# A two-layer token mixer with routed experts on one core: the router's ranks and gates for all tiles in one step, and the second layer's first modulation vectors computed behind the first layer's output projection

## The chip, the cores and the metric

One NeuronCore of a Trainium2 chip runs the whole program in one launch. The metric is the time of one execution on the device in microseconds (us), as the median of 3 runs. Engines are named as the profile names them: PE is the matrix engine (PEld its weight load), DVE, ACT and POOL are the vector, scalar and general engines, and SP is the engine whose queue issues every transfer from the chip's memory (HBM) into the on-chip memory (SBUF). Matrix results land in PSUM banks.

## The reference, cut to what matters

There are 256 context tokens and 256 latent tokens of width 1024, in four tiles of 128 tokens, and two layers. A layer first makes six modulation vectors per condition from `silu(c) @ w_mod + b_mod` (a matrix of 1024 x 6144, 24 MB, in chunks of 2048 columns: chunk 0 is shift and scale ahead of the mixer), then mixes tokens (layer 0: mLSTM and retention heads; layer 1: differential attention), projects out, and runs a mixture of experts. The router picks one of 4 groups and two of its 8 experts:

```python
u_lat = adaln(h_lat, norm1_g[l], m_lat[:, 0], m_lat[:, 1])     # chunk 0 of the layer's modulation
h_lat = h_lat + m_lat[:, 2] * y_lat                            # y_lat: the mixer's output projection
pg_top, grp = lax.top_k(softmax(x @ wg + bg), 1)               # one group of 4
pe_top, e_in = lax.top_k(softmax(le[grp]), TOP_K)              # two of its 8 experts
gate = pg_top * pe_top / sum(pe_top)
out[tok] += gate * ((silu(x @ w1[e]) * (x @ w3[e])) @ w2[e])   # 32 experts, 6 MB of weights each
```

All arithmetic is in float32. Each layer reads 192 MB of expert weights.

## The kernel before, in words

The program is written with four engine streams. A scheduler orders the instructions of the mixer stages; in `weave` (L183) a main task and side tasks are interleaved by estimated PE time, which sets the program order that the scheduler starts from. In the expert stages the PE order is the written one (`manual_schedule`). Each engine executes its own stream strictly in order, and so does SP's queue: a transfer that waits holds up all transfers behind it.

**Transfers.** `wslot` (L98) puts every 1 MB weight slice into a buffer of a ring. Ring a has three such buffers, and further rings (b, c, e) open when stages end. The list `slots` names the ring of the next slice. During the whole of layer 0 it is `[0, 0, 0]`, ring a. In the last part of layer 0, one of ring a's three buffers holds `vw`, the float32 router input of the last two tiles, so two are left.

**Modulation.** `mod_gen` (L219) takes eight slices of `w_mod` in turn; each needs four matmuls of 32 rows (`modps`, L226, 8 records in the trace), then one DVE addition of the bias (L230). `mod_cols` (L284) transposes the result (`modtp`) and copies shift and scale into `sh1` and `a11`. In layer 0 the generator `mods0` (L1316) makes chunks 1 and 2 and then chunk 0 of layer 1, one slice after every second step of the dense projections.

**Layer 0's end.** The output projection is done for the second half of the columns with one tile at a time (L1447; `oacc`, L954 to L956), while two tasks `Router.part` (tiles 0 and 1, then 2 and 3) add the result to the stream `h`, transpose it (`hpt`), compute the logits (`lgp`, L523), and pick groups and experts in some 25 short DVE operations (`first_max`) that end in the two-hot matrix `selb` (`go`, L561). `finish` (L580) turns it into ranks: 128x32 matmuls (`rank`) count earlier tokens of the same expert, DVE makes `pos`, and `gates` makes the gates. Tiles 0 and 1 are finished on their own, before tiles 2 and 3 have their logits.

**Experts.** `moe` (L629) prefetches 12 slices, then `prep` (L658) builds the 0/1 matrix `Pm` from `pos`, and `gather` (L670) multiplies it with the tokens to collect each expert's up to 64 tokens (`ga`; tiles 0 and 1 as a high and a low part, L683 and L684; tiles 2 and 3 of the first group of four experts in float32 from `vw`, L680). Before the change, `Pm` and the gather of tiles 0 and 1 for all four banks come first, and tiles 2 and 3 are added when their ranks are there. `up` (L828) multiplies with w1 and w3 (`f`, L844 and L846), with the gathers of banks 2 and 3 between the first expert's halves; `down` multiplies with w2 (`y`, L868), and the result is spread back (`sc`, L714 and L715). Two experts form a pair; 16 pairs make a layer.

Of the kernel before, what the change touches and what calls it, by code (L numbers as in the profile page):

```python
# [11 lines left out]
F32 = mybir.dt.float32  # L12
# [11 lines left out]
CAP = 64  # L24
# [50 lines left out]
def tile_backbone(ctx, tc, x, c, ctx_in, c_ctx, w_mod, b_mod, norm1_g, norm2_g, w_in_even, ml_gate_b,  # L75
# [361 lines left out]
    class Router:  # L437
# [37 lines left out]
        def part(self, i0, tiles, banks, m2, rows, pool, pp, lgp, vh, vl):  # L475
# [2 lines left out]
            m, q = len(tiles), 1 if tiles[0] < 2 else 0  # L478
            last = i0 + m == self.nt
            if i0 == 0:  # L480
                self.selb = go[:, 2:4, :].rearrange("p a b -> p (a b)").bitcast(BF16).rearrange("p (a b) -> p a b", b=32)
# [9 lines left out]
            def st(name, *shape, pool=pool):  # L491
                return pool.tile([128, m] + list(shape), F32, tag=f"r_{name}", name=name)
# [45 lines left out]
            def first_max(src, w, costs, oh, mx, which=ALU.is_equal):  # L538
# [3 lines left out]
                for i in range(m):  # L542
# [7 lines left out]
            eg = st("eg", 4, pool=keep)  # L550
# [8 lines left out]
            sel = gs[:, i0:i0 + m, :]  # L559
            selb = self.selb  # L560
            V.tensor_tensor(selb[:, i0:i0 + m, :], oh1, oh2, op=ALU.add)  # L561
# [3 lines left out]
            e = st("e", pool=keep)  # L565
            V.tensor_tensor(e, m2, m1, op=ALU.subtract)
            S.activation(e, e, AF.Exp)
            self.state = i0, m, sel, eg, e, oh1, oh2
# [10 lines left out]

        def finish(self, rk):  # L580

            i0, m, sel, eg, e, oh1, oh2 = self.state
            selb = self.selb
            last = i0 + m == self.nt
            for i in range(m):
                for q in range(i0 + i):
                    mm(rk[:, i, :], lhsT=ones_b.to_broadcast([128, 128]), rhs=selb[:, q, :], start=(q == 0), stop=False)
                mm(rk[:, i, :], lhsT=stri_b, rhs=selb[:, i0 + i, :], start=(i0 + i == 0), stop=True)
            if last:
                for i in range(self.nt):  # L590
                    mm(rk[:, m, :], lhsT=ones_b.to_broadcast([128, 128]), rhs=selb[:, i, :], start=(i == 0), stop=(i == self.nt - 1))
            gst, post, got = gs[:, i0:i0 + m, :], pos[:, i0:i0 + m, :], go[:, i0:i0 + m, :]
            V.scalar_tensor_tensor(post, rk[:, 0:m, :], 1.0, sel, op0=ALU.add, op1=ALU.mult)
            if last:
                V.tensor_scalar(ovf, rk[:, m, :], CAP + 0.5, None, op0=ALU.is_ge)

            def st(name):
                return keep.tile([128, m], F32, tag=f"r_{name}", name=name)

            def bc(ap):  # L600
                return ap.unsqueeze(2).to_broadcast([128, m, 32])

            def gates():
                zg = st("zg")
                V.tensor_reduce(zg, eg, axis=AX.X, op=ALU.add)
                g1 = st("g1")
                V.scalar_tensor_tensor(g1, e, 1.0, zg, op0=ALU.add, op1=ALU.mult)
                V.reciprocal(g1, g1)
                g2 = st("g2")
                V.tensor_tensor(g2, e, g1, op=ALU.mult)  # L610
                V.tensor_tensor(oh1, oh1, bc(g1), op=ALU.mult)
                V.tensor_tensor(oh2, oh2, bc(g2), op=ALU.mult)
                V.tensor_tensor(gst, oh1, oh2, op=ALU.add)
                V.scalar_tensor_tensor(got, post, CAP + 0.5, gst, op0=ALU.is_ge, op1=ALU.mult)

            if last:
                self.gates = gates
            else:
                gates()

    def row(vec, q, hl, pool, pp, name):

# [6 lines left out]
    def moe(l, tiles, rt, ahead):  # L629
# [25 lines left out]
        once.insert(9, extra.pop(l))  # L655
        once.insert(11, extra.pop())

        def prep(eg, part=slice(0, nt)):  # L658
            es = slice(4 * eg, 4 * eg + 4)
            if part.start == 0:  # L660
                sel[eg] = pool.tile([128, nt, 4, CAP], F32R, tag="Pm", bufs=1, name="Pm")
                xgs[eg] = pool.tile([128, 8, 4 * CAP], F32, tag=f"xg{eg % 2}", bufs=1, name="xg")
            n = part.stop - part.start
            return V.tensor_tensor(sel[eg][:, part], iota.unsqueeze(1).unsqueeze(1).to_broadcast([128, n, 4, CAP]),  # L664
                            pos[:, part, es].unsqueeze(3).to_broadcast([128, n, 4, CAP]), op=ALU.is_equal)

        def bank(shape, name):
            return pp.tile(shape, F32, tag="x", bufs=4, name=name)

        def gather(eg, kk, part=range(nt), pg=None):  # L670

            Pm, xg = sel[eg], xgs[eg]
            if pg is None:
                pg = bank([128, 2, 4 * CAP], "ga")
            for r in range(2):
                k = 2 * kk + r
                for i in part:
                    rhs = Pm[:, i].rearrange("p e s -> p (e s)")
                    if eg == 0 and i >= nt - 2:
                        mm(pg[:, r, :], lhsT=rt.v[:, i - nt + 2, k, :], rhs=rhs.bitcast(F32), start=(i == 0 and r == 0),  # L680
                           stop=(i == nt - 1 and r == 1))
                        continue
                    mm(pg[:, r, :], lhsT=vh[i][:, k, :], rhs=rhs, start=(i == 0 and r == 0), stop=False)  # L683
                    mm(pg[:, r, :], lhsT=vl[i][:, k, :], rhs=rhs, start=False, stop=(i == nt - 1 and r == 1))  # L684
            if nt - 1 in part:
                S.activation(xg[:, 2 * kk:2 * kk + 2, :], pg, AF.Copy)
            return pg

        def gated(p):

# [190 lines left out]

        order = pe_order()
        fetch(12)
        begun = [None] * 4
        if nt == 4:
            prep(0, slice(0, 2))
        rt.finish(pp.tile([128, 3, 32], F32, tag="f1", bufs=2, name="rank"))
        chosen = prep(0, slice(nt - 2, nt))
        if nt == 4:
            begun = [gather(0, kk, range(2)) for kk in range(4)]  # L890
        rt.gates()
        for kk in range(2):
            gather(0, kk, range(nt - 2, nt), begun[kk])
        pend = iter(())
        npair = NEXP // 2
        ng = npair // 2
# [414 lines left out]
    def z0(b):  # L1311
        return [(t0, zh[b], zl[b]) for t0 in (0, 128)]

    msb10 = modp.tile([128, 512], F32, tag="msb", name="msb10")

    def mods0():  # L1316
        yield from mod_gen(0, 1, modp, mpp, "mp", msb1)
        hl = split_rows(wsp, msb1, ("whi", "wlo"), 3)
# [119 lines left out]
    def late_rows():  # L1438
        for q in (1, 0):
# [4 lines left out]
            rows[q] = s2, row(4, q, hl, late, pp, f"a2{q}")  # L1444
            yield 0.5, 0.0, None

    weave(itertools.chain(*(out_proj(W, [(z0(0) + z0(1))[j]], accp, "acc", [banks[j]], kept=kept if j else None,  # L1447
                                     keeps=None if j else kept) for j in range(4))),
          ([late_rows()], 1),
          ([rt.part(0, (0, 1), banks, m2[0], lambda: rows.get(1), late, pp, lgp[:, 0:2], x8(0, 2), x8(2, 2)),  # L1450
            rt.part(2, (2, 3), banks, m2[1], lambda: rows.get(0), late, pp, lgp[:, 2:4], x8(1, 2), x8(3, 2))], 2))
# [264 lines left out]
```

## Time and profile before

| what | us |
|---|---|
| median of 3 runs (1610.06 to 1611.92) | 1611.63 |
| profiled execution, its own time | 1612.89 |
| its span, first to last instruction | 1611.0 |
| PE busy | 1511.6 (94%) |
| DVE busy | 710.4 (44%) |
| ACT busy | 490.3 (30%) |
| the transfers of the issuing queue, as a share of 16 DMA engines' span | 78.0% |

The mean granted PE clock is 0.981 of full speed. In the trace's timeline the layer 0 mixer ends at 383.4 us with the last `oacc` matmul; the first expert stage runs from there to 888, the second layer's mixer to 1120, and the second expert stage to the end. A PE that is shown busy need not be at its peak, since ends of matmuls are modelled: the distance between starts is the better measure. An engine's idle time is shown with what ended it ("<-"). Waits on SP's queue are waits before a transfer was issued; when it lands is read from the stretches in which bytes flow.

### The profile page before, as it was taken

To read this page: it belongs to the slowest core of one execution; us is meant where nothing else is said; L and a number is where in the kernel's file an instruction comes from. 1 tells how busy PE (TensorE), PEld (TensorE's weight loads), DVE (VectorE), ACT (ScalarE), POOL (GpSimd) and SP (SyncE) were. 2 spreads that over 40 slices of the span, in tenths; PEclk is the share of its full clock that TensorE was granted. 3 is DMA by queue.
4 is the path that set the end of the run, shared out by engine and by line. 5 is a ranking of instruction groups with operands and counts; after the bars stand their busy time and mean duration, and the time that the engine had idled before them with its cause. 6 is when DMAs were issued, how large, how long until landed. Compare 5 with 4: busy or idle time off the path is not lost. (4 is left out here: it accounts for less than half of the span.)

```text
span 1611.0 us, 19387 instructions
## 1 busy us (share of the span) xinstructions
PE 1511.6 (94%) x7354; PEld 833.7 (52%) x7354; DVE 710.4 (44%) x1496; ACT 490.3 (30%) x913; POOL 318.8 (20%) x287
## 2 busy tenths in 40 slices
PE   6999999997999999999998899999899999999985
PEld 4676666676545445454443556767434443433432
DVE  2345685577234445344343566565323232322323
ACT  3326563372211111111111567665212111111111
POOL 1100021000024334234243311001012121211212
PEclk9999999998999999999999999999899999999998
DMA  9554435324999999999997765227899999999994
GB/s 321 198 204 163 157 106 183 105 105 181 380 379 420 420 420 419 420 419 420 420 420 296 265 254 170 104 79 288 312 398 420 421 419 420 420 420 421 419 421 166
DMA packets 96682, 498.35 MB, mean 309 GB/s; under 512 B 14132, under 2 KB 22628, under 8 KB 42180
## 3 DMA queue, kind: packets, MB, share of 16 engines
q1 hardware_dynamic: 96580, 497.02, 78.0%
q8 instruction: 61, 1.00, 0.3%
q14 instruction: 41, 0.34, 0.1%
HBM read 495.94 MB, written 1.05 MB: 308 GB/s over the span
## 5 line engine op out<-in xcount | busy, mean ns | idle before, releaser
L846 PE MATMUL f<-w,xg 128*64 128x512 f32 x1024 | 450.8, 594 | 16.5 <-DMA w<-in_w_dram 16.5
L844 PE MATMUL f<-w,xg 128*64 128x512 f32 x1024 | 450.8, 593 | 0.0
L846 PEld LDWEIGHTS f<-w,xg 128*64 128x64 f32 x1024 | 137.6, 137 | 200.8 <-issue 161.0
L717 DVE TENSOR_TENSOR tmp<-sc,m 128x512 f32<-128x512 f32 x192 | 128.2, 688 | 253.8 <-PE sc L715 241.5
L718 POOL TENSOR_TENSOR h_lat<-h_lat,tmp 128x512 f32<-128x512 f32 x124 | 157.5, 1283 | 395.1 <-DVE tmp L717 391.5
L868 PE MATMUL y<-w,gT 128*64 128x512 f32 x1024 | 226.8, 595 | 0.0
L844 PEld LDWEIGHTS f<-w,xg 128*64 128x64 f32 x1024 | 137.8, 137 | 120.8 <-issue 117.7
L848 ACT ACTIVATE g<-f 64x512 f32<-64x512 f32 x64 | 37.9, 592 | 411.4 <-PE f L846 277.2
L395 DVE TENSOR_TENSOR wlo<-w,whi 128x512 fp32r<-128x512 f32 x136 | 98.9, 733 | 124.8 <-ACT whi L394 117.6
L718 POOL TENSOR_TENSOR h_ctx<-h_ctx,tmp 128x512 f32<-128x512 f32 x62 | 85.2, 1386 | 339.1 <-DVE tmp L717 338.0
L868 PEld LDWEIGHTS y<-w,gT 128*64 128x64 f32 x1024 | 70.6, 137 | 133.4 <-issue 131.3
L394 ACT ACTIVATE whi<-w 128x512 fp32r<-128x512 f32 x136 | 88.6, 658 | 144.3 <-PE dacc L426 88.3
L425 PE MATMUL dacc<-x,whi 128*128 128x512 f32 (+1 forms) x320 | 128.0, 403 | 3.9 <-DVE rq L1380 2.5
L849 DVE TENSOR_TENSOR g<-g,f 64x512 f32<-64x512 f32 x64 | 43.8, 685 | 194.5 <-ACT g L848 193.6
L427 PE MATMUL dacc<-x,wlo 128*128 128x512 f32 (+1 forms) x320 | 120.3, 378 | 2.0 <-DVE wlo L395 1.8
L426 PE MATMUL dacc<-x,whi 128*128 128x512 f32 (+1 forms) x320 | 120.0, 375 | 0.0
L878 DVE SCALAR_TENSOR_TENSOR yhl<-y,gsl,yhl 128x1024 fp32r<-128x1024 f32 (+1 forms) x34 | 41.5, 1221 | 138.4 <-ACT yhl L877 136.9
L877 ACT ACTIVATE yhl<-y,gsl 128x1024 fp32r<-128x1024 f32 (+1 forms) x34 | 36.2, 1064 | 205.9 <-PE y L868 204.2
L714 PE MATMUL sc<-yhl,Gm 128*128 128x512 f32 x192 | 83.7, 436 | 12.8 <-issue 12.4
L683 PE MATMUL ga<-Pm,x 128*128 128x256 f32 x352 | 88.7, 287 | 0.3 <-DVE Pm L664 0.3
L684 PE MATMUL ga<-Pm,x 128*128 128x256 f32 x352 | 88.0, 285 | 0.0
L695 DVE TENSOR_SCALAR Pg<-ca,pos,gs 128x64 f32<-128x64 f32 x192 | 79.7, 477 | 5.6 <-PE gg L702 5.6
(355 smaller groups left out, 2148.5 us busy)
## 6 DMA issues: line engine op xcount, KB each, us to landing
w<-in_w_dram SPq DMA_DIRECT2D x384, 1024.0 KB
w<-in_w_mod_dram SPq DMA_DIRECT2D x40, 1024.0 KB
w<-in_w_in_even_dram SPq DMA_DIRECT2D x16, 1024.0 KB
w<-in_w_in_odd_dram SPq DMA_DIRECT2D x12, 1024.0 KB
wm<-in_w_mod_dram SPq DMA_DIRECT2D x16, 512.0 KB
w<-in_w_out_even_dram SPq DMA_DIRECT2D x4, 1024.0 KB
w<-in_w_out_odd_dram SPq DMA_DIRECT2D x4, 1024.0 KB
cb<-in_consts_dram SPq DMA_DIRECT2D x1, 1344.0 KB
```

The lines of the kernel that those rows point to most:

```text
L394: S.activation(hi, w, AF.Copy)
L395: V.tensor_tensor(lo, w, hi.bitcast(F32), op=ALU.subtract)
L425: mm(d, lhsT=hi[:, sl], rhs=ah(k, ts), start=(k == 0), stop=False)
L426: mm(d, lhsT=hi[:, sl], rhs=al(k, ts), start=False, stop=False)
L427: mm(d, lhsT=lo[:, sl], rhs=ah(k, ts), start=False, stop=(k == 7))
L683: mm(pg[:, r, :], lhsT=vh[i][:, k, :], rhs=rhs, start=(i == 0 and r == 0), stop=False)
L684: mm(pg[:, r, :], lhsT=vl[i][:, k, :], rhs=rhs, start=False, stop=(i == nt - 1 and r == 1))
L717: V.tensor_tensor(tmp, sc, m5s[0][:, 1 if j < 2 else 0, hs], op=ALU.mult)
L718: (V if final and half else G).tensor_tensor(h[j][:, hs], h[j][:, hs], tmp, op=ALU.add)
L844: mm(f1[o1:o1 + 64, :], lhsT=xg[:, k, xsl], rhs=wa[:, kk, :], start=(k == 0), stop=(k == 7), tile_position=(0, o1))
L846: mm(f1[o3:o3 + 64, :], lhsT=xg[:, k, xsl], rhs=wb[:, kk, :], start=(k == 0), stop=(k == 7), tile_position=(0, o3))
L868: mm(y[64 * q:64 * q + 64, half, :], lhsT=gT[:, k, 64 * q:64 * q + 64], rhs=ws[q][:, r, 512 * half:512 * half + 512], start=(k == 0), stop ...
```

## The change

Two edits are made. First, the router: `part` no longer calls `finish`, and one `finish` after both parts makes ranks for all four tiles in one PSUM tile, one `pos`, one `Pm` for all tiles, and then the gates of all tiles, which are held behind `Pm` (`issue_after`). The one-hot matrices are written straight into `gs` and into a part of `go`, so that the second sum and some small operations go (12 DVE instructions fewer over both layers). The gather is no longer split into tiles 0 and 1 and tiles 2 and 3. Second, chunk 0 of layer 1's modulation leaves `mods0` and becomes `next_mods`, appended to the main task of the last weave, behind the four output projections.

```diff
         def part(self, i0, tiles, banks, m2, rows, pool, pp, lgp, vh, vl):
-            oh1, oh2 = st("oh1", 32, pool=keep), st("oh2", 32, pool=keep)
+            oh1, oh2 = gs[:, its], self.sec[:, its]
...
-            V.tensor_tensor(sel, oh1, oh2, op=ALU.add)
...
-            if not last:
-                self.finish(pp.tile([128, m + 1, 32], F32, tag="ps", name="rank"))
-                yield 0.4, 0.0, None
...
         def finish(self, rk):
+            nt, selb, eg, e = self.nt, self.selb, self.eg, self.e
+            for i in range(nt):
+                for q in range(i):
                     mm(rk[:, i, :], lhsT=ones_b.to_broadcast([128, 128]), rhs=selb[:, q, :], start=(q == 0), stop=False)
...
+            V.scalar_tensor_tensor(post, rk[:, 0:nt, :], 1.0, selb[:, 0:nt], op0=ALU.add, op1=ALU.mult)
...
         (moe)
-        begun = [None] * 4
-        if nt == 4:
-            prep(0, slice(0, 2))
-        rt.finish(pp.tile([128, 3, 32], F32, tag="f1", bufs=2, name="rank"))
-        chosen = prep(0, slice(nt - 2, nt))
-        if nt == 4:
-            begun = [gather(0, kk, range(2)) for kk in range(4)]
-        rt.gates()
+        rt.finish(pp.tile([128, nt + 1, 32], F32, tag="f1", bufs=2, name="rank"))
+        chosen = prep(0)
+        with tc.issue_after(chosen.ins):
+            rt.gates()
         for kk in range(2):
-            gather(0, kk, range(nt - 2, nt), begun[kk])
+            gather(0, kk)
...
         (mods0)
-        yield from mod_gen(1, 0, modp, mpp, "mp", msb10)
-        mod_cols(1, msb10, pp, "ps", sh1, a11)
-        yield 0.9
...
+    def next_mods():
+        msb = late.tile([128, 512], F32, name="msb10")
+        yield from mod_gen(1, 0, late, accp, "acc", msb)
+        mod_cols(1, msb, pp, "ps", sh1, a11)
+        yield 0.9
+
     weave(itertools.chain(*(out_proj(...) for j in range(4)), next_mods()),
```

On PE, at the end of layer 0's output projection, the rows before were these (`hpt` and `lgp` are the transposes and logits of the last two tiles, `rank` the rank matmuls):

```order
L956 MATMUL oacc<-wk,x_2731 128x512
L588 LDWEIGHTS stri_b
L588 MATMUL rank<-go,stri_b 128x32
L587 LDWEIGHTS ones_b
L587 MATMUL rank<-go,ones_b 128x32
L588 LDWEIGHTS stri_b
L588 MATMUL rank<-go,stri_b 128x32
L511 MATMUL hpt<-ca,h_lat 128x128 x8
L523 MATMUL lgp<-wr,hT 128x36 x8
L587 LDWEIGHTS ones_b
L587 MATMUL rank<-go,ones_b 128x32
```

At the same place on PE the changed kernel has:

```order
L930 MATMUL oacc<-wk,x_2665 128x512
L514 MATMUL hpt<-ca,h_lat 128x128 x4
L526 MATMUL lgp<-wr,hT 128x36 x4
L226 MATMUL modps<-w,cond 32x512 x32
L287 MATMUL modtp<-ca,msb_3228 128x128 x4
L582 LDWEIGHTS stri_b
L582 MATMUL rank<-go,stri_b 128x32
L581 LDWEIGHTS ones_b
L581 MATMUL rank<-go,ones_b 128x32
```

The rank matmuls of tiles 0 and 1 no longer stand ahead of the last tile's `hpt`; all 32 matmuls of the eight modulation slices and their transposes stand between the last logits and the first rank.

On SP's queue, before, the transfers around the end of layer 0 (`w_out_even` is the output projection, `w` from `w_dram` are expert slices; the brackets name the engines whose progress a transfer waits for) were these:

```order
L114 DMA w<-in_w_out_even_dram 128x4x512 [waits DVE_49]
L114 DMA w<-in_w_dram 128x2048 [waits DVE_49,PE_49,Pool_49]
L114 DMA w<-in_w_dram 128x2048 x2
L114 DMA w<-in_w_dram 128x2048 [waits DVE_49,PE_49]
L114 DMA w<-in_w_dram 128x2048 [waits DMAHW5_49,DVE_49]
L114 DMA w<-in_w_dram 128x2048 [waits DMAHW7_49,DVE_49]
L114 DMA w<-in_w_dram 128x2048 [waits DMAHW6_49,PE_49]
L114 DMA w<-in_w_dram 128x2048 [waits PE_49]
```

In the changed kernel SP's queue reads, from the last of the first four expert slices on:

```order
L114 DMA w<-in_w_dram 128x2048 [waits DMAHW3_49,DVE_49,PE_49]
L111 DMA w<-in_w_mod_dram 128x2048 [waits DMAHW4_49,DVE_49]
L111 DMA w<-in_w_mod_dram 128x2048 [waits DMAHW5_49,DVE_49]
L111 DMA w<-in_w_mod_dram 128x2048 [waits DMAHW6_49,DMAHW4_49,PE_49]
L111 DMA w<-in_w_mod_dram 128x2048 [waits DMAHW7_49,DMAHW5_49,PE_49]
L111 DMA w<-in_w_mod_dram 128x2048 [waits DMAHW6_49,DMAHW0_49,PE_49]
L111 DMA w<-in_w_mod_dram 128x2048 [waits DMAHW7_49,DMAHW1_49,PE_49]
L111 DMA w<-in_w_mod_dram 128x2048 [waits DMAHW2_49,DMAHW0_49,PE_49]
L111 DMA w<-in_w_mod_dram 128x2048 [waits DMAHW3_49,DMAHW1_49,PE_49]
L114 DMA w<-in_w_dram 128x2048 [waits DMAHW2_49,PE_49]
L114 DMA w<-in_w_dram 128x2048 [waits DMAHW3_49,PE_49]
L114 DMA w<-in_w_dram 128x2048 [waits DVE_49,Activation_49]
```

The eight modulation slices now stand behind the first four expert slices and ahead of all others. The first two go into the two free buffers of ring a; from the third on, each waits for PE to have multiplied the slice two places before it, and so do the two expert slices that follow.

## Rows read from the trace of the kernel before

**Rows 1.** Stages: busy time by engine (instructions), granted clock, DMA share, rate.
```profile
core 0: us, PE busy (x) PEld busy (x) DVE busy (x) ACT busy (x) POOL busy (x), PEclk, DMA share, GB/s
0.00:383.00 383.00, 364.42 (x1736) 251.18 (x1737) 214.70 (x582) 175.00 (x354) 40.47 (x68) 0.99 0.48 165
400.00:470.00 70.00, 69.78 (x356) 38.47 (x358) 25.04 (x55) 14.43 (x23) 11.00 (x8) 0.96 0.94 372
470.00:850.00 380.00, 379.45 (x1952) 184.58 (x1950) 162.72 (x265) 60.54 (x90) 135.74 (x104) 1.00 1.01 420
1135.00:1611.00 476.00, 437.38 (x2018) 183.57 (x2018) 136.41 (x215) 78.76 (x126) 83.15 (x65) 0.98 0.95 390
```

**Rows 2.** PE's waits, 470 to 850: us in total, times, longest.
```profile
PE gt L855 <- DVE tmp L717: 0.4, 1, 0.4
```

**Rows 3.** PE in time: a modulation slice and the transposes; then their count.
```profile
259.84 1.06 PE L226 MATMUL modps<-w,cond 128*32 128x512 f32 x8
260.83 0.50 PE L430 MATMUL dacc<-whi,x 128*128 128x512 f32 x1
303.51 0.60 PE L287 MATMUL modtp<-ca,msb 128*128 128x128 f32 x4
...
230.00:306.00 76.00, 10.60 (x64) 1.52 (x64) 1.00 0.50 166
```

**Rows 4.** PE in time, from the last output projection to the first expert.
```profile
383.00 0.40 PE L956 MATMUL oacc<-wk,x 128*128 128x512 f32 x1
387.99 1.79 PE L511 MATMUL hpt<-ca,h_lat 128*128 128x128 f32 x8
389.67 1.92 PE L523 MATMUL lgp<-wr,hT 128*128 128x36 f32 x8
399.06 0.18 PE L588 MATMUL rank<-go,stri_b 128*128 128x32 bf16 x1 [4.78 <-DVE go L561]
399.80 0.58 PE L683 MATMUL ga<-Pm,x 128*128 128x256 f32 x1 [0.34 <-DVE Pm L664]
406.12 3.61 PE L680 MATMUL ga<-Pm,vw 128*128 128x256 f32 x16
409.66 0.64 PE L844 MATMUL f<-w,xg 128*64 128x512 f32 x1
416.90 0.64 PE L844 MATMUL f<-w,xg 128*64 128x512 f32 x1
```

**Rows 5.** DVE in time: the last tile's stream, and a `Pm` of all tiles.
```profile
385.95 0.69 DVE L504 TENSOR_TENSOR h_lat<-v,h_lat 128x512 f32<-128x512 f32 x1
417.00 1.23 DVE L664 TENSOR_TENSOR Pm<-ca,pos 128x1024 fp32r<-128x1024 f32 x1 [11.24 <-PE ga L680]
```

**Rows 6.** SP's queue, 330 to 400: an issue, and its waits.
```profile
379.23 4.36 SPq L114 DMA_DIRECT2D w<-in_w_dram  x5
SPq L114 <- PE oacc L956: 39.6, 2, 39.1
```

**Rows 7.** One slice alone: its issue, and the stretch in which it ends.
```profile
304.87 0.37 SPq L114 DMA_DIRECT2D w<-in_w_out_even_dram  x1
309.00:310.00 1.00, 1.00 (x5) 0.75 (x4) 0.25 (x1) 0.69 (x2) 0.00 (x0) 1.00 0.29 109
```

**Rows 8.** Layer 1: three modulation slices after a pause, and SP's wait there.
```profile
892.75 4.48 PE L226 MATMUL modps<-w,cond 128*32 128x512 f32 x24 [4.01 <-DVE tmp L717]
SPq L111 <- PE modps L226: 5.1, 1, 5.1
```

**Rows 9.** Stretches: the clock around the router, and the first expert stage's end.
```profile
390.00:395.00 5.00, 3.54 (x18) 3.34 (x18) 2.09 (x11) 1.51 (x2) 0.00 (x0) 0.50 0.86 362
400.00:405.00 5.00, 5.00 (x24) 5.00 (x25) 5.00 (x19) 0.00 (x0) 0.00 (x0) 0.50 1.01 411
865.00:870.00 5.00, 4.45 (x23) 2.58 (x23) 3.67 (x7) 1.20 (x2) 4.85 (x5) 1.00 0.74 306
```

**Rows 10.** PE in time: the last slices of the first expert stage in use.
```profile
859.39 0.59 PE L846 MATMUL f<-w,xg 128*64 128x512 f32 x1
```

More of the change, by code (lines that the diff above doesn't have):

```diff
@@ L480, in part @@
             if i0 == 0:
-                self.selb = go[:, 2:4, :].rearrange("p a b -> p (a b)").bitcast(BF16).rearrange("p (a b) -> p a b", b=32)
+                self.sec, self.selb = (go[:, n:n + 2, :].rearrange("p a b -> p (a b)").bitcast(BF16)
+                                       .rearrange("p (a b) -> p a b", b=32) for n in (0, 2))
+                self.eg = keep.tile([128, self.nt, 4], F32, tag="r_eg", name="eg")
+                self.e = keep.tile([128, self.nt], F32, tag="r_e", name="e")
             vh, vl = (t.rearrange("p t (k q) -> p t k q", k=8) for t in (vh, vl))
@@ L549, in part @@
             first_max(lg[:, :, 0:4], 4, cost[:, 0:4], ohg, mg, ALU.is_lt)
-            eg = st("eg", 4, pool=keep)
+            its = slice(i0, i0 + m)
+            eg, e = self.eg[:, its], self.e[:, its]
             le = st("le", 32)
@@ L580, in finish @@
         def finish(self, rk):
[L582 to L586, printed above, removed]
-                    mm(rk[:, i, :], lhsT=ones_b.to_broadcast([128, 128]), rhs=selb[:, q, :], start=(q == 0), stop=False)
[L588 to L595, printed above, removed]
+            nt, selb, eg, e = self.nt, self.selb, self.eg, self.e
+            for i in range(nt):
+                for q in range(i):
+                    mm(rk[:, i, :], lhsT=ones_b.to_broadcast([128, 128]), rhs=selb[:, q, :], start=(q == 0), stop=False)
+                mm(rk[:, i, :], lhsT=stri_b, rhs=selb[:, i, :], start=(i == 0), stop=True)
@@ L597, in st @@
+            for i in range(nt):
+                mm(rk[:, nt, :], lhsT=ones_b.to_broadcast([128, 128]), rhs=selb[:, i, :], start=(i == 0), stop=(i == nt - 1))
+            gst, post, got = gs[:, 0:nt], pos[:, 0:nt], go[:, 0:nt]
+            V.scalar_tensor_tensor(post, rk[:, 0:nt, :], 1.0, selb[:, 0:nt], op0=ALU.add, op1=ALU.mult)
             def st(name):
-                return keep.tile([128, m], F32, tag=f"r_{name}", name=name)
-            def bc(ap):
-                return ap.unsqueeze(2).to_broadcast([128, m, 32])
+                return keep.tile([128, nt], F32, tag=f"r_{name}", name=name)
@@ L608, in gates @@
                 V.reciprocal(g1, g1)
[L609 removed]
                 V.tensor_tensor(g2, e, g1, op=ALU.mult)
[L611 to L613 removed]
+                V.tensor_tensor(gst, gst, g1.unsqueeze(2).to_broadcast([128, nt, 32]), op=ALU.mult)
+                for i in range(nt):
+                    V.scalar_tensor_tensor(gst[:, i], self.sec[:, i], g2[:, i:i + 1], gst[:, i], op0=ALU.mult, op1=ALU.add)
@@ L614, in gates @@
                 V.scalar_tensor_tensor(got, post, CAP + 0.5, gst, op0=ALU.is_ge, op1=ALU.mult)
[L616 to L619, printed above, removed]
+            self.gates = gates
     def row(vec, q, hl, pool, pp, name):
@@ L656, in moe, with prep @@
         once.insert(11, extra.pop())
-        def prep(eg, part=slice(0, nt)):
+        def prep(eg):
             es = slice(4 * eg, 4 * eg + 4)
[L660 to L665, printed above, removed]
+            sel[eg] = pool.tile([128, nt, 4, CAP], F32R, tag="Pm", bufs=1, name="Pm")
+            xgs[eg] = pool.tile([128, 8, 4 * CAP], F32, tag=f"xg{eg % 2}", bufs=1, name="xg")
+            return V.tensor_tensor(sel[eg], iota.unsqueeze(1).unsqueeze(1).to_broadcast([128, nt, 4, CAP]),
+                                   pos[:, 0:nt, es].unsqueeze(3).to_broadcast([128, nt, 4, CAP]), op=ALU.is_equal)
@@ L667, in bank, with gather @@
         def bank(shape, name):
             return pp.tile(shape, F32, tag="x", bufs=4, name=name)
-        def gather(eg, kk, part=range(nt), pg=None):
+        def gather(eg, kk):
             Pm, xg = sel[eg], xgs[eg]
-            if pg is None:
-                pg = bank([128, 2, 4 * CAP], "ga")
+            pg = bank([128, 2, 4 * CAP], "ga")
             for r in range(2):
                 k = 2 * kk + r
-                for i in part:
+                for i in range(nt):
                     rhs = Pm[:, i].rearrange("p e s -> p (e s)")
@@ L684, in gather @@
[L684 to L687, printed above, removed]
+                    mm(pg[:, r, :], lhsT=vh[i][:, k, :], rhs=rhs, start=(i == 0), stop=False)
+                    mm(pg[:, r, :], lhsT=vl[i][:, k, :], rhs=rhs, start=False, stop=(i == nt - 1))
+            S.activation(xg[:, 2 * kk:2 * kk + 2, :], pg, AF.Copy)
@@ L1312, in z0 @@
         return [(t0, zh[b], zl[b]) for t0 in (0, 128)]
-    msb10 = modp.tile([128, 512], F32, tag="msb", name="msb10")
     def mods0():
@@ L1445, in late_rows @@
             yield 0.5, 0.0, None
+    def next_mods():
[3 more added lines that the diff above has]
+        yield 0.9
     weave(itertools.chain(*(out_proj(W, [(z0(0) + z0(1))[j]], accp, "acc", [banks[j]], kept=kept if j else None,
-                                     keeps=None if j else kept) for j in range(4))),
+                                     keeps=None if j else kept) for j in range(4)), next_mods()),
           ([late_rows()], 1),
```

20 lines of the change are left out of this document (7 added, 13 removed).

## Prediction

> **What bounds the kernel now.** I read the stages first, then the waits of PE, then single stretches in order of time. In the stage table [rows 1] the reader is to see that layer 0's mixer keeps PE busy for 364 of 383 us while the transfers use half of their capacity (0.48, 165 GB/s): that stage is bound by PE. From 470 to 850 us, in the first expert stage, both are full: PE 379.45 of 380 us, DMA share 1.01 at 420 GB/s. In that stretch PE waits for no transfer at all; its only wait is 0.4 us for DVE [rows 2]. So PE bounds the first expert stage, and the transfers are close behind it. The second expert stage moves 390 GB/s with PE at 437 of 476 us [rows 1], so there the transfers are the limit. Between 383.4 and 399.8 us lies a stretch that neither covers: the out-projection ends (383.00 + 0.40), and PE does little until the first gather at 399.80, because it waits for the router's chain of small DVE operations [rows 4]. What the change puts into that stretch, and when the stretch begins, decides the time. All sums go by the profiled execution, whose 1612.89 us are 1.26 above the median of the runs; I take the difference to the median at the end.
>
> **The modulation slices leave layer 0.** A slice's four matmuls hold PE from 259.84 to the next instruction at 260.83, so 1.0 us, and there are 64 records, eight slices of 8; the transposes take 0.6 [rows 3]. That is 8 x 1.0 + 0.6 = 8.6, of which I count 8.5. PE bounds the stage, so out-projection and the DVE work that hangs on it should come 8.5 us earlier: its end moves from 383.4 to 374.9. PE is busy 95% of that stage, which would give 8.1; if DVE and ACT chains take PE's place for half of it, 4.2. I take 8.5 and keep 4.2 as the low end. The eight transfers, 20 us at 420 GB/s, were free there.
>
> **They come back in a place where nothing covers them.** PE takes them in order after the last tile's logits and before the first rank matmul, so the ranks, `pos`, `Pm`, every gather and the whole expert stage queue behind them. On SP's queue they stand behind an expert slice that waits for an out-projection matmul: in the kernel before, that was issued at 379.23 after a wait of 39.1 us [rows 6], now 8.5 earlier, at 370.7. Two modulation slices follow at once into ring a's two free buffers and are there by 380. The third waits for PE to finish the first, the fourth for the second, and so on, and all expert slices but four wait behind them.
>
> When does PE reach the first? The last tile's `h_lat` was ready at 386.64 (385.95 + 0.69) [rows 5]. The new DVE order has two more logit operations ahead of it (0.5), so 387.1 - 8.5 = 378.6. From the start of `hpt` to the start of the logits it was 1.7 us (387.99 to 389.67) and the logits took 1.9 [rows 4]; that gives 382.2. The earlier rank of tiles 0 and 1, for which the last `hpt` waited, is gone, which is in these numbers.
>
> A slice's matmuls cost 1.0 us at the full clock [rows 3]. After a pause of 4.01 us in layer 1, three slices took 4.48, so 1.5 each, the clock being down at their start [rows 8]. Around the router the granted clock is 0.50 from 390 to 405 [rows 9], that is 1.2 GHz, after PE had idled from 383.4 on, and here PE will have idled likewise from 374.9. At half clock throughout it would be 2.0. I take 1.5, the row nearest to it. A single slice issued at 304.87 still flows for 0.29 of the stretch 309 to 310 [rows 7]: 4.4 us from issue to landing. With 0.2 for the hand-over, each buffer turns once in 4.4 + 0.2 + 1.5 = 6.1 us. The first slice is multiplied by 382.2 + 1.5 = 383.7. Slices three, five and seven follow it in three turns; the eighth comes 2.5 later, since two slices in flight share the channel (1 MB at 420 GB/s): 383.7 + 18.3 + 2.5 = 404.5. Layer 1's own row shows the same pattern: a modulation transfer there waited 5.1 us for `modps` on PE [rows 8].
>
> The Trainium skill, page "TensorE: Matmul & The Clock Gate", section "HAM oscillation — how this bites in real kernels", speaks against this place: where a matmul burst is shorter than the wait for the next transfer, the engine falls back to its slow state and every burst starts slow again. By that rule all slices would take 2.0 us, the sum below would be 2 to 3 us higher, and the row of layer 1 (1.5) agrees with it half way.
>
> **From the last slice to the first expert.** DVE adds the bias (0.7, as a 128x512 operation in [rows 5]), PE transposes (0.6 to 1.2, I take 0.9), the ranks took 0.4 of the 0.74 from 399.06 to 399.80 [rows 4], `pos` about 0.2, and `Pm` is now of all tiles at once, 1.23 [rows 5]; with 0.4 for hand-overs 3.8. The first gather starts at 408.3 instead of 399.80: +8.5. The router's DVE chain, 399.0 before, is done by about 387 and hidden behind the slices.
>
> Before, the 32 short gathers of tiles 0 and 1 ran from 399.80 to 406.12, at half clock until about 405 [rows 4, 9], and the float32 ones of two banks until 409.66; at full clock they are 32 x 0.12 = 3.8 and 3.5. Now only 16 short ones (1.9) precede the first expert, so 5.4 us at full clock; with the first 5.3 at half clock, as before, 8.0, not 9.9. The first expert starts at 416.3. Between its halves lay 7.24 us (409.66 to 416.90); the other 16 short gathers move in there: 9.1. The second half starts at 425.4 instead of 416.90: **+8.5**. The cover that the split gave (gathers of tiles 0 and 1 while DVE finished the others) was worth about the 1.2 of `Pm`, and is in the sum.
>
> **The transfers.** Ahead of the experts' slices now lie 8 MB more, and they resume only when PE has used the last modulation slices, about 404. Before, three slices had landed early, 5.9 until 400, and 24.8 from 400 to 470 (372 GB/s x 70 us, 1.05 MB each): 33.7. Now four, and 66 / 2.5 = 26 more: 30. The lag is 3.7 x 2.5 = 9 us at 470. At the end of the stage the channel empties at about 869 (0.74 of 865 to 870 [rows 9]); the last five slices before that, four of w2 and one of the next layer, are 12.5 us, so the last of w1 and w3 landed near 857, and PE wanted it at 859.39 [rows 10]. The margin is 2 to 4 us, and PE is itself 8.5 later. The lag uses 5 to 7 of that, so PE stays the bound.
>
> **Layer 1's router** loses a few operations of 0.1 to 0.2 us from a chain of which the rank wait hides most, and the overflow count reaches SP about 0.5 later. From -0.5 to +0.5; I take 0. The gates, later now, feed only the spreading back, 20 us on.
>
> **Sum.** 1612.89 + 8.5 = 1621.4 for the profiled execution, 1611.63 + 8.5 = 1620.1 against the median.
>
> **Rivals.**
> *The clock holds.* If PE stays at 2.4 GHz (slices 1.0, logits and transposes half): logits end at 380.6, the first slice at 381.6, the eighth at 381.6 + 3 x 5.6 + 2.5 = 400.9, the gather at 404.1, the expert at 409.5, its second half at 418.6: +1.7, 1613.3. For it: the first two slices are one dense run of matmuls, and the clock rose at 405 in such a run. Against it: the same pauses lowered it [rows 8, 9]. Chance 0.16.
> *The transfers become the bound.* From 400 to 470 they lost 8 us to waits for free buffers (372 against 420 GB/s [rows 1]). I counted that as made up. If it is lost again, the lag is 17, less 3 of margin: +14, 1625.5. It decides once the rate after resumption is under some 395 GB/s. Against it: the queue now has more free buffers than it can fill. Chance 0.12.
> *The slices do hide: faster.* If all eight were in SBUF when PE is done with the logits, they would fill PE's idle time: end at 382.2 + 12 = 394.2 or, at full clock, 388.6; then the second half at 415.1 or 406.3, so -1.8 to -10.6, middle -6.2: 1605.4. For it: 9.7 us of that stretch are idle before. It decides from six slices landed by 382 on. Against it: only two buffers are free, and the queue's third slice waits for PE. Chance 0.08.
>
> **The numbers.** The forecast has 0.64 and its own range, 1616 to 1624 (a slice at 1.2 to 2.0 us, the layer 0 gain 6 to 8.5). Less than 0.2%, 3.2 us, can't be told from no change. Slower: forecast and second rival, 0.76; same: the first rival, 0.16; faster: the third, 0.08. The range 1612 to 1626 leaves out the third rival, the low edge of the first and the high edges of the others, about 0.18; a layer 0 gain of 4.2 alone would give 1624.4.
>
> **What would show it.** Right: the out-projection ends near 375; `modps` comes in bursts some 3 us apart, each behind a transfer, until about 404, with a clock mostly near 0.5; the first gather near 408 and the second half of the first expert near 425; the expert slices' transfers pause between 380 and 404. Wrong: `modps` in one dense run before 395, an out-projection end at 380 or later, or PE waits for expert slices between 470 and 850.

## The result, and the profile after

The changed kernel takes 1620.57 us in the median (1620.04 to 1621.62, 4 runs) against 1610.85 of the kernel before beside it: the ratio is 1.0063, with a 95% interval of 1.0045 to 1.008. It is slower by some 9.7 us. The profiled execution took 1621.62 us, with a span of 1619.8.

The stages of the changed kernel come first (columns as in [rows 1]: the stretch, its length, then busy time and instructions of PE, PEld, DVE, ACT and POOL, the granted clock, the DMA share, the rate).

```profile
382.00:406.00 24.00, 11.61 (x48) 1.21 (x48) 3.50 (x15) 0.20 (x1) 0.00 (x0) 0.54 0.82 305
430.00:470.00 40.00, 39.78 (x213) 19.63 (x210) 10.79 (x21) 9.55 (x16) 4.16 (x4) 1.00 1.01 420
470.00:850.00 380.00, 379.56 (x1956) 185.42 (x1954) 162.90 (x265) 60.31 (x90) 135.19 (x104) 1.00 1.01 419
```

From 382 to 406 PE is busy for less than half of the time and DVE for 3.5 us: this is the new hole. From 430 on PE is as full as before, and the transfers are full from there, where before they became full at 470. What fills the hole is seen on PE in order of time. The columns are start, duration, line and operation, output <- inputs, and in brackets the idle time before it and what ended that.

```profile
374.93 0.40 PE L930 MATMUL oacc<-wk,x 128*128 128x512 f32 x1
377.09 0.63 PE L514 MATMUL hpt<-ca,h_lat 128*128 128x128 f32 x4 [1.77 <-DVE go L548]
378.74 1.08 PE L526 MATMUL lgp<-wr,hT 128*128 128x36 f32 x8 [1.02 <-ACT hT L523]
379.75 1.92 PE L226 MATMUL modps<-w,cond 128*32 128x512 f32 x16
385.65 1.94 PE L226 MATMUL modps<-w,cond 128*32 128x512 f32 x8 [3.97 <-DMA w<-in_w_mod_dram]
388.11 1.93 PE L226 MATMUL modps<-w,cond 128*32 128x512 f32 x8 [0.53 <-DMA w<-in_w_mod_dram]
392.58 1.94 PE L226 MATMUL modps<-w,cond 128*32 128x512 f32 x8 [2.54 <-DMA w<-in_w_mod_dram]
395.04 1.94 PE L226 MATMUL modps<-w,cond 128*32 128x512 f32 x8 [0.52 <-DMA w<-in_w_mod_dram]
399.56 1.93 PE L226 MATMUL modps<-w,cond 128*32 128x512 f32 x8 [2.58 <-DMA w<-in_w_mod_dram]
403.34 1.94 PE L226 MATMUL modps<-w,cond 128*32 128x512 f32 x8 [1.85 <-DMA w<-in_w_mod_dram]
406.09 1.12 PE L287 MATMUL modtp<-ca,msb 128*128 128x128 f32 x4 [0.81 <-DVE msb L230]
...
409.22 0.58 PE L663 MATMUL ga<-Pm,x 128*128 128x256 f32 x1 [1.64 <-DVE Pm L646]
...
417.31 0.64 PE L822 MATMUL f<-w,xg 128*64 128x512 f32 x1
...
426.44 0.64 PE L822 MATMUL f<-w,xg 128*64 128x512 f32 x1
```

Two slices run back to back (x16) and at the full clock, 1.92 us for both. Each of the other six waits for its transfer and takes twice as long. SP's queue shows the same from the side of the transfers (start of the first, time until the last was issued, count), and DVE that nothing else is late:

```profile
369.67 27.69 SPq L111 DMA_DIRECT2D w<-in_w_mod_dram  x8
401.55 35.77 SPq L114 DMA_DIRECT2D w<-in_w_dram  x19
```

```profile
384.92 0.23 DVE L563 TENSOR_TENSOR go<-gs,go 128x64 bf16<-128x64 f32 x1
405.34 0.69 DVE L230 TENSOR_TENSOR msb<-modps,modbias 128x512 f32<-128x512 f32 x1 [20.19 <-PE modps L226]
```

The last `go`, for which the ranks waited before [rows 4], is there at 385.15; then DVE idles for 20.19 us until the last slice is multiplied. The delay that stands at the second half of the first expert (416.90 before [rows 4], 426.44 now, +9.5) stays: the last `y` of the first expert stage starts at 878.48 instead of 868.96, the first `f` of the second stage at 1150.14 instead of 1140.64. The last `y`, before and after:

```profile
868.96 7.09 PE L868 MATMUL y<-w,gT 128*64 128x512 f32 x32
878.48 7.09 PE L846 MATMUL y<-w,gT 128*64 128x512 f32 x32
```

### The profile page after: what moved, and what is told of

The parts are those of the page before. It is cut to its first block, busy times and chain, and to the rows that moved or that the text cites. A ratio compares the mean times of both kernels' runs of the same rounds, so it can differ in the third digit from the quotient of the medians.

```text
span 1619.8 us, 19376 instructions
## 1 busy us (share of the span) xinstructions
PE 1510.9 (93%) x7354; PEld 831.4 (51%) x7354; DVE 710.5 (44%) x1485; ACT 489.7 (30%) x913; POOL 318.8 (20%) x287
```

## The experiments

Each run was timed beside the kernel before (its medians lay between 1611.1 and 1611.5 us). "Second half" is the start of the second half of the first expert, the mark used in the prediction.

| run | us | ratio to before, 95% interval | second half | last `y` of stage 1 |
|---|---|---|---|---|
| before, changed | 1610.85, 1620.57 | 1.0063 (1.0045 to 1.008) | 416.90, 426.44 | 868.96, 878.48 |
| router alone | 1607.31 | 0.9977 (0.9968 to 0.9986) | 411.78 | 863.82 |
| slices alone | 1628.34 | 1.0091 (1.0076 to 1.0107) | 431.01 | 883.49 |
| no slices | 1598.80 | 0.9916 (0.9903 to 0.993) | 405.19 | 857.26 |
| half transfers | 1614.93 | 1.0023 (1.0014 to 1.0032) | 420.59 | 872.63 |
| spare matmuls | 1619.40 | 1.0066 (1.0052 to 1.008) | 424.95 | 877.01 |
| two behind | 1608.28 | 0.9981 (0.9972 to 0.999) | 411.89 | 865.26 |
| four behind | 1607.28 | 0.9978 (0.9969 to 0.9987) | 408.19 | 864.48 |
| five behind | 1609.52 | 0.9987 (0.9978 to 0.9996) | 407.04 | 863.92 |
| five buffers | 1613.57 | 1.0014 (1.0005 to 1.0023) | 406.20 | 867.07 |
| late rank | 1607.82 | 0.9978 (0.9968 to 0.9988) | 410.99 | 863.03 |

**Router alone.** The slices go back into `mods0`:

```diff
+        yield from mod_gen(1, 0, modp, mpp, "mp", msb10)      # mods0
+        mod_cols(1, msb10, pp, "ps", sh1, a11)
...
-    weave(itertools.chain(*(out_proj(...) for j in range(4)), next_mods()),
+    weave(itertools.chain(*(out_proj(...) for j in range(4))),
```

> The router's part of the change alone: chunk 0 of layer 1's modulation stays in layer 0's dense projections. Theory A (the moved slices are the whole loss; the one-step router itself gains): in the changed kernel the last `go` ended 9.8 us after the last output projection, against 15.6 in the kernel before, and the first gather followed the rank by 2.2; so the first gather at 383.4 + 9.8 + 2.3 = 395.5, the second half of the first expert 17.2 later at 412.7 instead of 416.90: -4.2, about 1606.7 us. Theory B (as the prediction counted it: the lost split costs 1.2 and the shorter DVE chain is worth about as much): 1611 to 1612. Theory C (the one-step router is part of the loss): 1613 or more.

Theory A held: 1607.31 us, faster than the kernel before by 4.0. PE in the router's stretch:

```profile
382.55 0.40 PE L930 MATMUL oacc<-wk,x 128*128 128x512 f32 x1
384.69 0.63 PE L514 MATMUL hpt<-ca,h_lat 128*128 128x128 f32 x4 [1.75 <-DVE go L548]
386.07 1.92 PE L526 MATMUL lgp<-wr,hT 128*128 128x36 f32 x8 [0.75 <-ACT hT L523]
...
392.82 0.18 PE L582 MATMUL rank<-go,stri_b 128*128 128x32 bf16 x1 [4.70 <-DVE go L563]
```

The last `hpt` starts 2.1 us behind the start of the projection's last matmul (384.69 against 382.55), where it was 5.0 before (387.99 against 383.00 [rows 4]), and the rank of the last tiles comes 6.2 earlier. Before, eight `hpt` stand together at 387.99, those of tiles 2 and 3; here four are left, for tile 2 is done by then.

**Slices alone.** The old router, with `next_mods` behind the output projections (the bias tile takes the sum, for want of room):

```diff
-        yield from mod_gen(1, 0, modp, mpp, "mp", msb10)      # mods0
-        mod_cols(1, msb10, pp, "ps", sh1, a11)
...
+    weave(itertools.chain(*(out_proj(...) for j in range(4)), next_mods()),
```

> The moved modulation slices alone, with the router as it was before (ranks and gates in two steps, gather split into tiles 0-1 and 2-3). Theory A (the slices are the whole loss, since the ranks wait behind them in either form): last `modps` near 405, 1620 to 1622 us. Theory C (the one-step router is part of the loss): 1612 to 1616.

It took 1628.34 us, past every figure named; by the ratio that is 12.2 to 17.2 us more than before. Its times lie between 1623.4 and 1629.0 us and the trace is of 1628.4 us, so marks read from it are good to a few us only. At the second half the two edits nearly add up: slices +14.1, router -5.1, both +9.5. So the slices cost some 14 us with either router (14.7 with the new one), and the router gives back some 5 in either place. The medians of the runs with the new router agree: 1620.57 less 1607.31 is 13.3. How the router does so behind the slices stands on PE:

```profile
379.17 0.21 PE L588 MATMUL rank<-go,stri_b 128*128 128x32 bf16 x1 [4.49 <-DVE go L561]
...
381.15 1.92 PE L1448 MATMUL modps<-w,cond 128*32 128x512 f32 x2
...
388.57 1.94 PE L1448 MATMUL modps<-w,cond 128*32 128x512 f32 x8
...
408.98 1.94 PE L1448 MATMUL modps<-w,cond 128*32 128x512 f32 x8 [0.97 <-DMA w<-in_w_mod_dram]
```

The rank of tiles 0 and 1 waits 4.49 us for DVE, and the last `hpt`, the logits and the slices queue behind it. The clock has fallen by then, so the first two slices take 1.9 each too, and the last one starts at 408.98, where the changed kernel has 403.34. Theory A's figure was low because it took the slices to start at the same time in either form.

**No slices.** `next_mods` without its eight transfers and 32 matmuls:

```diff
-        yield from mod_gen(1, 0, late, accp, "acc", msb)
+        bias = mod_bias(1, 0, late)
+        V.tensor_copy(msb, bias)
+        state["slot"] += 8
```

> The changed kernel without the eight slices: nothing of w_mod is read or multiplied for chunk 0 of layer 1, the vectors are made of the bias alone (that part of the computation is left out). It gives the price of the slices where they now stand, and the most that hiding them could give. Theory A: output projection ends at 375.3 as in the changed kernel, the last `go` at 385.2, the first gather at 387.5, the second half of the first expert at 404.7 instead of 416.90: -12.2, about 1599 us. Theory D (behind an earlier PE the transfers become the bound of the first expert stage): 1603 to 1608, and PE waits for expert slices in that stage.

1598.80 us, as Theory A had it: the slices cost 21.8 us where they now stand (21.3 at the second half), and beside the router alone 8.5 us in the dense projections (6.6 at the second half). Theory D failed: the last `y` follows the second half as before (452.1 us behind it), so an earlier start alone doesn't make the transfers the bound.

**Half transfers.** The two places in the loop over the slices that differ:

```diff
...
-            w = mod_slice(1, 0, k)
+            w = rings[0].tile([128, 2048], F32, tag="w", name="w")[:, 0:1024]
+            nc.sync.dma_start(w, wv[:, k, 0:1024])
...
-                   rhs=w[:, 512 * g:512 * (g + 1)]
+                   rhs=w[:, 512 * (g % 2):512 * (g % 2) + 512]
```

> The changed kernel with each of the eight modulation transfers halved (128x1024 instead of 128x2048; the four matmuls of a slice use the same half twice, so half of the columns of the chunk is left out), PE's work as it was. Theory A (the price is the turn of two buffers: two slices land in 5.0 us, then PE takes 1.94 each at half clock): a turn of two slices falls from 6.95 to 2.5 + 1.94 = 4.4 us, three turns and the last slice end 7 to 8 us earlier, near 398: about 1613 us. Theory E (PE's own time at half clock and the handing over are the price): within 2 us of 1620.6.

```profile
389.61 3.64 PE L1426 MATMUL modps<-w,cond 128*32 128x512 f32 x16 [2.67 <-DMA w<-in_w_mod_dram]
396.53 3.64 PE L1426 MATMUL modps<-w,cond 128*32 128x512 f32 x16 [3.29 <-DMA w<-in_w_mod_dram]
```

1614.93 us: 5.6 of the 21.8 us went. The total is near Theory A's 1613, but the turn that it forecast didn't come: the last two pairs start 6.92 us apart (389.61, 396.53), as in the changed kernel, and not 4.4. Nor did the run change the bytes alone. On PE two slices stand ahead of the logits (377.11 and 379.52), and on SP's queue three whole expert slices were issued among the halves (371.28, 381.57, 387.38). The last slice ends 5.1 us earlier (400.17 against 405.28), 3.1 of which are there at the third (382.55 against 385.65). How much of this the bytes are worth, this run does not show, so it does not decide between A and E.

**Spare matmuls.** Behind the second to the seventh slice:

```diff
...
+            if 1 <= k < 7:
+                for n in range(8):
+                    mm(fill, lhsT=xv[:, 0, :], rhs=xv[:, 0:4, :], start=True, stop=True)
```

> The changed kernel with eight spare 128x512 matmuls on PE (operands in SBUF, result used nowhere) behind each of the second to seventh modulation slice, 0.23 us each at the full clock. In the changed kernel slices 3 to 8 took 1.94 us each at a granted clock of 0.50, and two slices turned in 6.95 us. Theory F (half of PE's clock is a part of the price, and it is down because PE pauses for the transfers): the clock stays near full, a slice takes 1.0, a turn 6.0, and the first gathers run at full clock: second half of the first expert at 421 to 423 instead of 426.44, 1615 to 1617 us. Theory G (the clock doesn't rise with them): the spare matmuls take 0.45 each, 3.6 behind a slice, a turn grows to 11 us, 1630 us or more.

```profile
388.99 1.06 PE L1425 MATMUL modps<-w,cond 128*32 128x512 f32 x8
389.99 2.57 PE L1429 MATMUL fill<-x 128*128 128x512 f32 x10
392.48 1.07 PE L1425 MATMUL modps<-w,cond 128*32 128x512 f32 x8
...
395.52 1.07 PE L1425 MATMUL modps<-w,cond 128*32 128x512 f32 x8
398.35 1.06 PE L1425 MATMUL modps<-w,cond 128*32 128x512 f32 x8 [1.76 <-DMA w<-in_w_mod_dram]
401.50 1.93 PE L1425 MATMUL modps<-w,cond 128*32 128x512 f32 x8 [2.09 <-DMA w<-in_w_mod_dram]
```

```profile
382.00:406.00 24.00, 19.08 (x113) 9.29 (x112) 3.03 (x15) 0.20 (x1) 0.00 (x0) 0.87 0.88 310
```

Theory F held for the clock: from 382 to 406 the granted clock is 0.87, against 0.54 of the changed kernel in the same stretch, and seven of the eight slices take 1.0, where in the changed kernel two do. So it was PE's pauses that held the clock down. It failed for the time: 1619.40 us, 1.2 less than the changed kernel (1.5 at the second half), which the intervals can't tell from nothing, and not 4 to 6. But the run can't price the clock. A slice and its spare matmuls hold PE for 3.49 us (388.99 to 392.48), so two take 7.0, as long as the turn of 6.95 that a faster slice was to shorten; the spare work took the place of the doubled time. And the projection ends 1.2 earlier here (374.10 against 375.33), which is most of the 1.5. What the half clock costs stays open. From the changed kernel's rows it can be estimated: a slice of 1.0 instead of 1.94 would take 0.94 off each of three turns and off the last slice, some 4 us of the 21.8.

**Two, four and five slices behind**, on the new router; the others stay in `mods0`, where their sum is kept in `msb10`. Only the number and the buffers differ (0 is ring a, 1 ring b, 2 ring c):

```diff
...
+        once.extend([0, 0])              # four: [1, 1, 0, 0]; five: [1, 1, 2, 0, 0]
+        yield from mod_slices(1, 0, range(6, 8), ps)      # range(4, 8); range(3, 8)
+        V.tensor_tensor(msb10, ps, msb10, op=ALU.add)
```

> The one-step router, six of the eight slices in layer 0's dense projections as before and only the last two behind the output projection, in ring a's two free buffers. Theory H (a slice behind the projection is free as long as it is in SBUF before PE has done the logits): layer 0 gains 2 x 1.0, the two slices run right behind the logits and end before DVE's last `go`, so the second half of the first expert comes 2 us earlier than with the router alone (411.78): 409.8, and 1605.3 us against 1607.3. Rival I (two expert slices come later, and the first expert or the stage waits for them): 1607 to 1611.

> As the run with two slices behind, but with four, in two buffers of ring b (free some 40 us before the end of the projection) and ring a's two free ones; the expert slices that were prefetched there come behind them. Theory H: second half of the first expert at 411.8 - 4 = 407.8, 1603.3 us. Rival I: PE waits for expert slices behind 400, or the transfers become the bound of the first expert stage: 1606 or more.

> As the run with four, but with five slices behind the projection; the fifth in the free buffer of ring c, so that all five are in SBUF before the logits. Theory H: second half of the first expert at 406.8, 1602.3 us. Rival I: PE waits for expert slices behind 400, or the transfers become the bound of the first expert stage: 1606 or more.

Theory H, that a slice in SBUF before the logits is free, held at the second half for four and five slices (408.19 and 407.04; 407.8 and 406.8 were expected), not for two (411.89). With two, the projection ended only 0.8 earlier than with the router alone, and the sum and the transposes moved in front of the ranks. Yet no run can be told to be faster than the router alone: at four and five rival I decided, and at two there was no gain at the second half to lose. The last two `y` of the first expert stage, with five behind, and the waits of PE and of its weight load for transfers in that stage (total, times, longest):

```profile
833.70 7.09 PE L855 MATMUL y<-w,gT 128*64 128x512 f32 x32
863.92 7.09 PE L855 MATMUL y<-w,gT 128*64 128x512 f32 x32
```

```profile
PE f L833 <- DMA w<-in_w_dram: 2.1, 3, 1.3
PEld f L833 <- DMA w<-in_w_dram: 4.8, 3, 2.2
```

With the router alone these two starts are 26.79 us apart, PE has no such wait and PEld 0.3 us for this `f`; here they are 30.22 apart. With four behind they are 29.88 apart, with two 28.13. From the second half to the last `y` it is 452.0 us with the router alone, and 453.4, 456.3 and 456.9 with two, four and five behind. With five, the 4.9 us more match the 4.8 in PEld's list: the transfers that the slices pushed back come short at the end of the stage, and the gain at its start is gone. In the three profiles layer 1's mixer is longer too: from the last `y` to the first `f` of the second expert stage it is 271.4 us with the router alone, and 273.0, 273.0 and 275.4. In each, the clock from 926 to 960 is 0.95 instead of 1.00; why it fell there, and how much of the difference it is, stays open.

**Five buffers.** The changed kernel with two lines more:

```diff
+        once.extend([1, 1, 2, 0, 0, 1, 1, 2])
+        state["slot"] += 8
         yield from mod_gen(1, 0, late, accp, "acc", msb)
```

> The changed kernel, all eight slices behind the output projection, but five buffers for them instead of two: ring b's two, the free one of ring c and ring a's two; the last three slices go into the first three of these again. Theory A (two buffers that turn are the price of the place): five slices are in SBUF before the logits and end near 382, the last three follow by about 390, the second half of the first expert starts at 410 to 412 instead of 426.44. Theory J (the transfers of the first expert stage then bound it: with five slices behind, the last `y` stood at 863.9 and waited for transfers; three more are 7.5 us): last `y` near 870, 1611 to 1614 us. Without J: last `y` near 853, 1605 us. If the buffers are not the price: second half at 420 or later, 1615 or more.

```profile
374.29 1.90 PE L226 MATMUL modps<-w,cond 128*32 128x512 f32 x10
...
378.81 3.63 PE L226 MATMUL modps<-w,cond 128*32 128x512 f32 x30
384.59 1.92 PE L226 MATMUL modps<-w,cond 128*32 128x512 f32 x16 [2.15 <-DMA w<-in_w_mod_dram]
...
867.07 7.09 PE L846 MATMUL y<-w,gT 128*64 128x512 f32 x32
```

```profile
PEld f L824 <- DMA w<-in_w_dram: 8.4, 12, 2.2
```

This is the test of the mechanism. With three more buffers the eight slices are done by 386.5 instead of 405.3, most at the full clock and the first ahead of the logits, and the second half comes 20.2 us earlier than in the changed kernel. Only 7.0 us of these arrive at the end. Theory J held: from 400 to 860 the transfers run at 420 GB/s without a break, and from the second half to the last `y` it takes 460.9 us, 8.8 more than in the changed kernel; 8.4 us stand in PEld's list as waits for expert slices. Layer 1's mixer takes another 3.4 (275.0 against 271.7 from the last `y` to the first `f`), with the clock at 0.95 from 926 to 960, as in the runs above.

**Late rank.** The kernel before; the finish of tiles 0 and 1 is held until the logits of tiles 2 and 3 are issued:

```diff
...
             if not last:
+                mine = self.state
+                yield 0.0, 0.0, "logits"
+                keepst, self.state = self.state, mine
                 self.finish(pp.tile([128, m + 1, 32], F32, tag="ps", name="rank"))
+                self.state = keepst
```

> The kernel before with one thing moved: the ranks and gates of tiles 0 and 1 are made only when the logits of tiles 2 and 3 have been issued, so that no rank matmul stands on PE ahead of the last tile's `hpt`; the two-step router, its split gather and the place of the modulation slices stay. Theory K (the one-step router gains because PE no longer waits with the last `hpt` for DVE's `go` of tiles 0 and 1): first rank of the last two tiles at 393 to 395 instead of 399.06, second half of the first expert at 411 to 413, 1606 to 1609 us. Theory L (the gain comes from the DVE operations and the second sum that went): 1610.5 us or more.

```profile
378.29 0.63 PE L511 MATMUL hpt<-ca,h_lat 128*128 128x128 f32 x4 [0.33 <-DVE le L555]
379.68 1.06 PE L523 MATMUL lgp<-wr,hT 128*128 128x36 f32 x8
...
384.67 0.63 PE L511 MATMUL hpt<-ca,h_lat 128*128 128x128 f32 x4 [1.76 <-DVE oh L548]
...
386.05 1.92 PE L523 MATMUL lgp<-wr,hT 128*128 128x36 f32 x8 [0.35 <-ACT hT L520]
...
393.10 0.18 PE L595 MATMUL rank<-go,stri_b 128*128 128x32 bf16 x1 [5.08 <-DVE go L564]
```

```profile
383.85 0.68 DVE L504 TENSOR_TENSOR h_lat<-v,h_lat 128x512 f32<-128x512 f32 x1
```

The kernel before had at these places, beside [rows 4, 5], tile 2's `h_lat` and tile 3's logits:

```profile
379.90 0.69 DVE L504 TENSOR_TENSOR h_lat<-v,h_lat 128x512 f32<-128x512 f32 x1
```

```profile
392.33 1.90 PE L523 MATMUL lgp<-wr,hT 128*128 128x36 f32 x8 [0.74 <-DVE go L614]
```

Theory K held: 1607.82 us. The old router, with its split gather and all its DVE operations, is as fast as the new one once the ranks of tiles 0 and 1 are made later. So the gain of the new router comes from the order, not from the operations that went. The rank matmuls had held up both last tiles: tile 2's `h_lat` was ready at 380.59, its `hpt` ran at 387.99; now it runs at 378.29, and its logits are out of the way. That is some 2.9 of the 6.0 us by which the first rank of the last tiles comes earlier (from `hpt` to the end of the logits 6.2 before, 3.3 now). Of the 3.3 at the last `hpt` only 1.2 are PE's own delay behind `h_lat`; the other 2.1 are `h_lat` itself, ready at 384.53 instead of 386.64, since the DVE order changed with the edit. How much of the gain belongs to PE's order and how much to DVE's, the run does not separate.

## Why the prediction was right, step by step

The forecast was 1620.1 us; the sum's mark, the second half, was 425.4 and is 426.44. The mechanism was the one forecast, but several terms were off and cancelled.

- **Layer 0's gain, 8.5.** The projection ends at 375.33 instead of 383.40: 8.1. Of these 0.45 are the router's (it ends at 382.95 with the router alone), so the slices' part is 7.6; even the 8.1 from PE's share of 95%, which I put aside for 8.5, was a little high. The no-slices run gives 6.6 to 8.5.
- **The logits' end, 382.2.** It is 379.75. Two terms failed. The start of the last `hpt` was put at 378.6 and is 377.09: from the projection's end to `h_lat` it took 3.24 us before (383.40 to 386.64), the sum added 0.5, and it took 1.61 (375.33 to 376.94). And the logits were put at 1.9, taken from a stretch at a clock of 0.50 [rows 4, 9]; here they take 1.08, at the full clock. The 1.7 from `hpt` to the logits came out (1.65) by luck: in the row it was eight transposes one behind another, here it is four and a wait of 1.02 for ACT. "Is in these numbers" was half right: the sum set the last `hpt` 0.9 earlier than its row at 387.99, and the late rank is worth 3.3 there (384.67).
- **A slice, 1.5; a turn of each buffer, 6.1.** The first two took 1.0, the other six 1.94, and a turn took 6.95 (385.65 to 392.58, 388.11 to 395.04). I had taken the row of layer 1 [rows 8]. The rule of the Trainium skill ("TensorE: Matmul & The Clock Gate", section "HAM oscillation — how this bites in real kernels") is that a burst shorter than the wait for its next transfer starts slow each time. Three of the six rows agree with it (waits of 3.97, 2.54 and 2.58 us); the other three are as slow behind waits of 0.53, 0.52 and 1.85, shorter than their bursts. By that rule the mark would have been put 2 to 3 us later, at about 428, 1.5 too late. No run shows what the clock by itself cost: the spare matmuls lifted it but took the time that it gave back.
- **The last slice.** Forecast at 404.5, it ends at 405.28: the first slice is done 3.0 us earlier than forecast (380.7 against 383.7), three turns take 2.5 more, and the eighth comes 3.8 behind the seventh instead of 2.5.
- **From there to the second half.** 3.8, 8.0 and 9.1 were forecast; 3.94, 8.09 and 9.13 are measured.
- **The transfers.** PE stayed the bound of the first expert stage, as forecast: from the second half to the last `y` it is 452.0 us, 452.1 before. That the margin is small is confirmed by the runs with slices in more buffers: there the last `y` stops following the second half, between 863.9 and 867.1.
- **The rivals.** The slices hide only where they have buffers (five buffers, four and five behind), which was that rival's condition; two were free. The clock fell, as the forecast said. The transfers did not become the bound in the changed kernel, but in its mended form they did.
- **What the prediction missed.** It read the eight `hpt` of [rows 4] as the last tile's, where half are tile 2's, held up by the same rank matmuls. So it valued the router edit at nothing beyond the lost split, and put the whole loss, 8.5, on the slices. The router is a gain of 5.1 at the second half (4.0 in the median), and the slices a loss of 14.1. The total came out by luck: the earlier first slice (3.0) and the longer turns with the late last slice (3.8), both missed, are about equal. The total alone would not have shown it; the run with one edit did.

The best versions run are the router edit alone, four slices behind in four buffers, and the kernel before with the late rank: 1607.3, 1607.3 and 1607.8 us, with intervals that overlap.

## What to carry to other kernels

Work that is moved into an engine's idle time is free only with its operands there: count the buffers that are free at that place, and if fewer than the transfers, price each further filling of the buffers at a whole turn (transfer, use, hand-over; 6.95 us for two slices here), not at the engine's share. Look at what stands on an in-order engine behind an instruction that waits for another engine: rank matmuls placed too early, with the DVE order that came of it, cost some 4 us. Where the engine and the transfers are both full in the next stage, bytes that are pushed into it have to be paid there: the early start without the slices was kept to the end of the stage, nearly the same start with the slices in five buffers lost 8.8 us of it there.

## What the runs showed of the hardware

PE's clock in a stretch of short bursts can be held up by useless matmuls: from 382 to 406 it is 0.87 with them, 0.54 without. A full PE line can hide a wait: with five behind PE's own list has 2.1 us of waits for expert slices in the first expert stage, its weight load's 4.8, and the stage is 4.9 longer. That the same three slices of layer 1 took 4.48 us after a pause of 4.16 us (changed kernel), 4.43 after 2.73 (router alone) and 2.78 after 3.57 (two behind) I had not expected: the length of the pause alone does not decide at which of the two levels they run.
